# Output projection, second norm, queries and scores of a transformer-like block, cut into two halves of 256 tokens

## The chip, the cores and the metric

One core of one Trainium2 chip runs the whole block. The metric is the device time of one execution in microseconds (us). Its engines are TensorE (PE; PEld is its loading of weights), VectorE (DVE), ScalarE (ACT), GpSimd (POOL) and SyncE (SP), which issues most DMA transfers. Each works through its own list of instructions in order and waits for the others by semaphores.

## The reference

One layer on 512 tokens of width 1024, in float32. Cut to what this change touches:

```
y = concat([head_rmsnorm(y_a), head_rmsnorm(y_b)]) @ w_out     # output projection
x = x + g1 * y
h = modulate(rmsnorm(x, norm2_g), sh2, sc2)                    # second norm
q = (h @ w_q).reshape(p, 8, 2, 64)                             # queries: 8 heads, 2 halves of 64
sc = einsum('phcd,hcnd->phcn', q, sub_keys)                    # scores against 128 keys per half
top_s, top_i = top_k(sc, 16)                                   # stage 1 of the search
best_s, best_pos = top_k(all sums of a pair of them, 16)       # stage 2
idx = the 16 of 16384 experts per token and head;  g = softmax(best_s)
act = gelu(einsum('phkd,pd->phk', expert_u[idx], h))
x = x + g2 * einsum('phk,phkd->pd', g * act, expert_v[idx])
out = rmsnorm(x, final_g)
```

## The kernel before

Tokens stand in four tiles of 128. Activations are transposed: a tensor is [128 features, 8 blocks k, 512 tokens]. Each float32 product is made of three fast ones: `split_w` turns a 512 KB weight block (`wraw`) into a rounded part (`whi`, ACT, L76) and its remainder (`wlo`, DVE, L81), and `mm3` (L90 to L92) issues for each k whi times the rounded activation, whi times its remainder, and wlo times the rounded activation: 24 matmuls for a block. `wraw`, `whi` and `wlo` have four buffers each.

The program has these stages.

1. The mixer (to about 188 us), which this change leaves alone. It ends in `ybuf_h` and `ybuf_l`, the input of the output projection.
2. Output projection: a loop over 8 blocks m of features, 24 matmuls of 512 tokens each; DVE adds to the residual `xs` (L388); ACT squares it (L162) and DVE sums the squares (L164).
3. Second norm: PE sums the squares over the features (L154), `rsqrt_small` (L111 to L117, DVE and ACT) makes 1/rms, PE spreads it over the partitions (`ps_rs`, L172), and for each k DVE multiplies (L434), `modulate` scales and shifts (DVE L213, ACT L214, DVE L215), and PE transposes the result of tile 0 and of the first 64 tokens of tile 1 (L423, L425) to `h2n` and `h2b`, which the gathered tokens need. Meanwhile `xs` is transposed (L399) and stored for the end.
4. Queries and scores: a loop over 8 heads h, 24 matmuls of 512 tokens, an eviction of the query (`qT`, ACT L484), 8 score matmuls (L488) and two evictions of the scores (`sc`, ACT L494). DVE starts the searches of stage 1 there (`top16`, L451 to L460; one tile of one head is one item): heads 0 to 3, all four tiles, 16 items.
5. The u phase: 124 of 128 chunks of `expert_u`, 24 matmuls of 320 tokens each (`ps_act`, L90 to L92), ACT evicting with Gelu (L817). These are the dense tokens, 64 to 128 of tile 1 and tiles 2 and 3. Tile 0 and the first 64 tokens of tile 1 are instead gathered: POOL fetches the 128 rows of one chosen expert per token (L729, 512 KB), and DVE makes one "dot" of it (L750); 64 dots for tile 1 (index `idx_b`), then 128 for tile 0 (index `idx_s`). The other 16 items of stage 1, stage 2 (`topk_tile`) and the "gates" (which put the weights of the chosen experts in the dense layout: DVE L605 and L615, ACT L613, PE L621, 96 steps) run beside the chunks.
6. The v phase: the last four u chunks among 128 chunks of `expert_v`, 18 matmuls of 512 columns each (L996); beside them the dots that are left and 128 sums of gathered `expert_v` rows (DVE L766).
7. The end: the gated residual and the final norm.

Up to the end of stage 4 the order on each engine is made by a scheduler from the program's text. From stage 5 on it is a list made in Python (`manual_schedule`): a planner keeps estimated times of PE, DVE and ACT (`pe[0]`, `dve[0]`, `ac[0]`), and in each chunk lets `turn` choose pieces of searches ("s", "r"), gates ("g") and dots ("d") until DVE's estimate reaches PE's. Dots of tile 0 wait until `topk_tile(0)` has been placed (`sready`, L746), which comes after `topk_tile(1)`, the rest of stage 1, and `topk_tile(2)`. In the v phase, `share` spreads the steps that are left evenly over the chunks, whatever their number.

## Time and profile before

| | us |
|---|---|
| median of 3 runs | 1409.85 (1409.26 to 1412.09) |
| the profiled execution | 1409.24 |
| its span, from first to last instruction | 1407.5 |
| around the span | 1.74 |

| engine | busy us | share of the span |
|---|---|---|
| PE | 1357.2 | 96% |
| PEld | 1176.0 | 84% |
| DVE | 1231.5 | 87% |
| ACT | 735.2 | 52% |
| POOL | 540.1 | 38% |

The DMA queues moved 440.10 MB. Busy shares are means over stages with different limits, and a busy PE is not a PE at its peak, since a matmul's recorded length (390 ns at 512 columns) is longer than the distance between two of them (227 ns). So the prediction goes by starts, and by stage.

### The profile page before, as it was taken

The numbers are of one execution on the slowest core, as the hardware profiler recorded it, in microseconds if no ns is written. First come the engines' busy times: TensorE is split into PE (matmuls) and PEld (weight loads), VectorE is DVE, ScalarE is ACT, GpSimd is POOL, SyncE is SP. The second block draws the span as 40 slices with busy tenths as digits, with TensorE's granted clock in tenths as the row PEclk, the third lists the DMA queues.
The fourth block names the chain that finished last, engine by engine and source line by source line (L and its number), as shares of the span: only waits on it lengthen the run. The fifth ranks groups of instructions, "written<-read, shape, count | busy, mean of one in ns | idle before, by whom it ended". The sixth has DMA issues, their size and how long they took to land.

```text
span 1407.5 us, 22023 instructions
## 1 busy us (share of the span) xinstructions
PE 1357.2 (96%) x7739; PEld 1176.0 (84%) x7739; DVE 1231.5 (87%) x2470; ACT 735.2 (52%) x1212; POOL 540.1 (38%) x334
## 2 busy tenths in 40 slices
PE   5999998999999999999999989999999999999996
PEld 2566777779999999999999988877778888878884
DVE  6676565799999999989999967989989898999998
ACT  3554433536489699956996533333333333343342
POOL 0000000000135434514333335666757676766770
PEclk9999999999999999999999999999999999999998
DMA  9575323124689899978999899999999999999994
GB/s 378 213 256 197 132 85 103 53 91 138 206 273 406 320 346 367 391 251 309 353 369 373 301 402 383 368 359 413 410 413 414 415 412 415 414 407 413 414 369 177
DMA packets 146931, 440.10 MB, mean 313 GB/s; under 512 B 14722, under 2 KB 42370, under 8 KB 144772
## 3 DMA queue, kind: packets, MB, share of 16 engines
q1 hardware_dynamic: 99812, 267.75, 51.4%
q0 software_dynamic: 46720, 169.89, 31.5%
q8 instruction: 61, 1.00, 0.3%
q10 hardware_dynamic: 288, 1.05, 0.2%
q14 instruction: 50, 0.41, 0.1%
HBM read 393.54 MB, written 45.09 MB: 312 GB/s over the span
## 4 chain that ended last, share of the span: by engine, by line
PE 32%; issue 24%; DMA 20%; DVE 16%; POOL 6%; ACT 1%; DVEq 0%; POOLq 0%; SPq 0%; ACTq 0%
DMA wraw<-in_v_dram 13%; PE acc L996 7%; POOL rows L729 6%; PE ps_z L90 5%; PE ps_z L92 5%; PE ps_z L91 5%; DMA rows<-in_u_dram,idx_s 3%; DVE wlo L81 3%; DVE scr L750 3%; DVE ys L766 3%; DMA rows<-in_u_dram,idx_b 2%; PE ps_act L90 2%; DVE cf L882 2%; PE ps_act L91 2%; PE ps_act L92 2%
## 5 line engine op out<-in xcount | busy, mean ns | idle before, releaser
L76 ACT ACTIVATE whi<-wraw 128x1024 fp32r<-128x1024 f32 x292 | 308.4, 1057 | 392.9 <-DMA wraw<-in_v_dram 170.0
L81 DVE TENSOR_TENSOR wlo<-wraw,whi 128x1024 fp32r<-128x1024 f32 x292 | 356.1, 1221 | 82.5 <-ACT whi L76 81.3
L90 PE MATMUL ps_act<-h,whi 128*128 128x320 f32 x1024 | 322.4, 315 | 1.5 <-ACT sc L494 1.2
L91 PE MATMUL ps_act<-h,whi 128*128 128x320 f32 x1024 | 317.0, 310 | 0.0
L92 PE MATMUL ps_act<-h,wlo 128*128 128x320 f32 x1024 | 316.8, 309 | 0.0
L729 POOL DMA_INDIRECT rows<-in_u_dram,idx_s x128 | 201.1, 1571 | 226.5 <-DVE scr L750 187.3
L729 POOL DMA_INDIRECT rows<-in_v_dram,idx_s x128 | 234.7, 1833 | 108.9 <-DVE ys L766 82.1
L996 PE MATMUL acc<-whi,cl 128*128 128x512 f32 x750 | 232.7, 392 | 6.1 <-DVE cl L893 6.1
L996 PE MATMUL acc<-whi,ch 128*128 128x512 f32 x750 | 232.8, 391 | 5.2 <-ACT act L817 3.9
L996 PE MATMUL acc<-wlo,ch 128*128 128x512 f32 x750 | 232.0, 390 | 0.0
L90 PEld LDWEIGHTS ps_act<-h,whi 128*128 128x128 f32 x1024 | 193.0, 189 | 2.1 <-ACT sc L494 1.4
L91 PEld LDWEIGHTS ps_act<-h,whi 128*128 128x128 f32 x1024 | 193.0, 189 | 0.2
L92 PEld LDWEIGHTS ps_act<-h,wlo 128*128 128x128 f32 x1024 | 192.7, 188 | 0.0
L729 POOL DMA_INDIRECT rows<-in_u_dram,idx_b x64 | 99.2, 1550 | 211.7 <-DVE scr L750 105.6
L996 PEld LDWEIGHTS acc<-whi,cl 128*128 128x128 f32 x750 | 140.5, 189 | 38.8 <-DVE cl L893 10.2
L996 PEld LDWEIGHTS acc<-whi,ch 128*128 128x128 f32 x750 | 141.0, 188 | 35.7 <-ACT act L817 4.7
L996 PEld LDWEIGHTS acc<-wlo,ch 128*128 128x128 f32 x750 | 141.4, 189 | 29.7
L766 DVE SCALAR_TENSOR_TENSOR ys<-rows,acts,ys 128x1024 f32<-128x1024 f32 x127 | 162.8, 1282 | 1.6
L750 DVE SCALAR_TENSOR_TENSOR scr<-rows,h2n 128x1024 f16<-128x1024 f32 x128 | 156.4, 1222 | 8.2 <-DMA rows<-in_u_dram,idx_s 6.7
L406 POOL DMA_DIRECT2D x1d<-xn x8 | 4.6, 569 | 282.5 <-DVE wlo L81 234.9
L817 ACT ACTIVATE act<-ps_act 128x320 f32<-128x320 f32 x128 | 55.4, 433 | 102.3 <-PE ps_act L92 100.4
L621 PE MATMUL ps_gt<-igh,jh 128*128 128x128 f32 x768 | 97.4, 275 | 2.6 <-DVE igh L615 0.9
(258 smaller groups left out, 1888.4 us busy)
## 6 DMA issues: line engine op xcount, KB each, us to landing
wraw<-in_uT_dram SPq DMA_DIRECT2D x128, 512.0 KB, 6.8
wraw<-in_v_dram SPq DMA_DIRECT2D x128, 512.0 KB, 10.1
Gd<-stg SPq DMA_DIRECT2D x46, 512.0 KB, 7.0
wada<-in_w_ada_dram SPq DMA_DIRECT2D x16, 1024.0 KB, 5.3
Ad<-act SPq DMA_DIRECT2D x48, 320.0 KB, 7.7
act<-Ad SPq DMA_DIRECT2D x48, 320.0 KB, 11.4
h<-Gd SPq DMA_DIRECT2D x12, 1024.0 KB, 17.7
wraw<-in_w_in_dram SPq DMA_DIRECT2D x20, 512.0 KB, 6.0
```

Of the source, the lines that this page charges most:

```text
L76: nc.scalar.activation(hi, raw, AF.Copy)
L81: nc.vector.tensor_sub(lo, raw, hi.bitcast(F32))
L90: nc.tensor.matmul(ps, hi[:, k, :], xh(k), start=first and k == ks[0], stop=False)
L91: nc.tensor.matmul(ps, hi[:, k, :], xl(k), start=False, stop=False)
L92: nc.tensor.matmul(ps, lo[:, k, :], xh(k), start=False, stop=last and k == ks[-1])
L621: nc.tensor.matmul(pg[:, :, k], jh[:, k, :], ig[:, k, :], start=True, stop=True)
L729: nc.gpsimd.indirect_dma_start(out=r[:, :], out_offset=None, in_=table, in_offset=bass.IndirectOffsetOnAxis(ap=idxs[:, k:k + 1], axis=0))
L750: nc.vector.scalar_tensor_tensor(scr, rows.pop(n), 1.0, hn, op0=OP.mult, op1=OP.mult, accum_out=dst[:, k:k + 1])
L766: nc.vector.scalar_tensor_tensor(ys, rows.pop(k), acts[:, k:k + 1], ys, op0=OP.mult, op1=OP.add)
L817: nc.scalar.activation(act[c // 2][:, c % 2], ps, AF.Gelu)
L882: nc.vector.tensor_mul(cf[:, :, XB:].rearrange("p c (g t) -> p c g t", t=16), act.pop(vorder[2 * q] // 2).rearrange("p c (g t) -> p c g t" ...
L996: nc.tensor.matmul(accs[b][e], st[:, bs], mv[:, e * 512:(e + 1) * 512], start=first, stop=last)
```

## The change

- The tokens are cut into two halves of 256 (tiles 0 and 1, tiles 2 and 3). The output projection runs over all 8 blocks for half 0, then over all 8 for half 1. `w_out` is loaded and split twice.
- Statistic, 1/rms and modulation are made for each half. Those of half 0 are written in the text before the projection of half 1, those of half 1 before the queries.
- Queries and scores go in 16 steps of one head and 256 tokens: heads 0 to 3 of half 0, heads 0 to 3 of half 1, then the same for heads 4 to 7. `w_q` is split once: four heads' weights are kept for both halves.
- The 16 items searched during the queries are now tiles 1 and 0 of all eight heads, one item after each step from the second on. In the u phase `topk_tile(1)` comes first, and the rest of stage 1 is tiles 2 and 3 of all heads.
- The scores have a pool for each half, and no buffer of theirs is used twice. The pool `ring` moves to the other side of SBUF.

In the diff's core, lines of "..." mark what is left out:

```diff
-    def modulate(t1, k, A, B, hh, hl, full=None):
-        f = sq_pool.tile([128, T], F32, name="mfull")
+    def modulate(t1, k, A, B, hh, hl, full=None, cols=slice(0, T)):
+        f = sq_pool.tile([128, T], F32, name="mfull")[:, 0:cols.stop - cols.start]
         nc.vector.tensor_scalar(f, t1, A[:, k:k + 1], B[:, k:k + 1], op0=OP.mult, op1=OP.add)
-        nc.scalar.activation(hh[:, k, :], t1, AF.Identity, scale=A[:, k:k + 1], bias=B[:, k:k + 1])
-        nc.vector.tensor_sub(hl[:, k, :], f, hh[:, k, :].bitcast(F32))
+        nc.scalar.activation(hh[:, k, cols], t1, AF.Identity, scale=A[:, k:k + 1], bias=B[:, k:k + 1])
+        nc.vector.tensor_sub(hl[:, k, cols], f, hh[:, k, cols].bitcast(F32))
...
-    oraw = {0: load_w(w_out[0]), 1: load_w(w_out[1])}
-    for m in range(KB):
-        if m + 2 < KB:
-            oraw[m + 2] = load_w(w_out[m + 2])
-        hi, lo = split_w(oraw[m])
-        ps = psZ.tile([128, T], F32, name="ps_z", bufs=3)
-        mm3(ps, hi, lo, lambda k: ybuf_h[:, k, :], lambda k: ybuf_l[:, k, :], kord, True, True)
-        nc.vector.scalar_tensor_tensor(xs[:, m, :], ps, adac[:, 16 + m:17 + m], xs[:, m, :], op0=OP.mult, op1=OP.add)
-        sq_sum(m, True)
-    mx.close()
-    adx.close()
-    qp = pro.enter_context(tc.tile_pool(name="qp", bufs=2))
+    HT = T // 2
+    half_cols = [slice(HT * e, HT * (e + 1)) for e in range(2)]
+    oraw = {i: load_w(w_out[i]) for i in range(2)}
     x1d = dram.tile([T, D], F32, name="x1d")
+    rstd2 = const.tile([128, NT], F32, name="rstd2")
+    A2 = const.tile([128, KB], F32, name="A2")
+    h2n = persist.tile([128, D], F32, name="h2n")
+
+    def half_stat(pst, src, o, first, last):
+        for t in range(2):
+            nc.tensor.matmul(pst[:, t:t + 1], src[:, o + t * 128:o + (t + 1) * 128], ones,
+                             start=first and t == 0, stop=last and t == 1, skip_group_check=True)
+
+    def out_half(e):
+        cs_ = half_cols[e]
+        for m in range(KB):
+            i = KB * e + m
+            if i + 2 < 2 * KB:
+                oraw[i + 2] = load_w(w_out[(i + 2) % KB])
+            hi, lo = split_w(oraw.pop(i))
+            ps = psZ.tile([128, T], F32, name="ps_z", bufs=3)[:, 0:HT]
+            mm3(ps, hi, lo, lambda k: ybuf_h[:, k, cs_], lambda k: ybuf_l[:, k, cs_], kord, True, True)
+            xm = xs[:, m, cs_]
+            nc.vector.scalar_tensor_tensor(xm, ps, adac[:, 16 + m:17 + m], xm, op0=OP.mult, op1=OP.add)
+            if m == 0:
+                nc.scalar.activation(sqa[:, cs_], xm, AF.Square)
+                continue
+            sq = sq_pool.tile([128, T], F32, name="sq")
+            nc.scalar.activation(sq[:, 0:HT], xm, AF.Square)
+            if m < KB - 1:
+                nc.vector.tensor_add(sqa[:, cs_], sqa[:, cs_], sq[:, 0:HT])
+        pst = psA.tile([128, NT], F32, name="ps_col")[:, 0:2]
+        half_stat(pst, sqa, HT * e, True, False)
+        half_stat(pst, sq, 0, False, True)
+        rs = rstd2[:, 2 * e:2 * e + 2]
+        rsqrt_small(rs, pst, 1.0 / D, 2)
+        psr = psA.tile([128, T], F32, name="ps_rs")[:, 0:HT]
+        rows_of(psr, rs, 2)
+        return psr
...
-    rstd2 = const.tile([128, NT], F32, name="rstd2")
-    rsqrt_small(rstd2, pst, 1.0 / D, NT)
-    x1p = [x1_mm(0)]
-    psr2 = psA.tile([128, T], F32, name="ps_rs")
-    rows_of(psr2, rstd2)
-    x1p += [x1_mm(1), x1_mm(2)]
-    A2 = const.tile([128, KB], F32, name="A2")
-    nc.vector.scalar_tensor_tensor(A2, adac[:, 32:40], 1.0, sm("n2g"), op0=OP.add, op1=OP.mult)
-    h2n = persist.tile([128, D], F32, name="h2n")
-    sel = ctx.enter_context(tc.tile_pool(name="sel", bufs=1, side="right"))
-    h2b = sel.tile([128, D], F32, name="h2b")
+    def norm_half(e, psr, full):
+        for k in range(KB):
+            t1 = sq_pool.tile([128, T], F32, name="mt1")[:, 0:HT]
+            nc.vector.tensor_mul(t1, xs[:, k, half_cols[e]], psr)
+            modulate(t1, k, A2, adac[:, 24:32], h2h, h2l, full, half_cols[e])
...
     tp_cur = []
+    psr = out_half(0)
+    nc.vector.scalar_tensor_tensor(A2, adac[:, 32:40], 1.0, sm("n2g"), op0=OP.add, op1=OP.mult)
+    h2b = sel.tile([128, D], F32, name="h2b")
+    norm_half(0, psr, full2)
+    psr = out_half(1)
+    mx.close()
+    qp = pro.enter_context(tc.tile_pool(name="qp", bufs=2))
     qraw = {0: load_w(w_q[0]), 1: load_w(w_q[1])}
-    for k in range(KB):
-        t1 = sq_pool.tile([128, T], F32, name="mt1")
-        nc.vector.tensor_mul(t1, xs[:, k, :], psr2)
-        modulate(t1, k, A2, adac[:, 24:32], h2h, h2l, full2)
-        if k < 3:
-            x1_out(*x1p[k])
+    norm_half(1, psr, None)
     ep = ExitStack()
-    ring = ctx.enter_context(tc.tile_pool(name="ring", bufs=1, side="right"))
     scp = ep.enter_context(tc.tile_pool(name="scp", bufs=1, side="right"))
     top = scp.tile([128, NT, 8, 2, 16], F32, name="top")
     ti = scp.tile([128, NT, 8, 2, 16], U32, name="ti")
     scx = ExitStack()
-    scs = scx.enter_context(tc.tile_pool(name="scs", bufs=1, side="right"))
+    scs = [pro.enter_context(tc.tile_pool(name="sca", bufs=1)),
+           scx.enter_context(tc.tile_pool(name="scb", bufs=1, side="right"))]
...
-    def stage1(heads, tiles):
-        for t in tiles:
-            for h in heads:
-                yield from top16([(top[:, t, h, c], ti[:, t, h, c], sc[h, c][:, t, :]) for c in range(2)], 128, 1150)
+    def stage1(items):
+        for t, h in items:
+            yield from top16([(top[:, t, h, c], ti[:, t, h, c], sc[h, t // 2][:, c, t % 2, :]) for c in range(2)], 128, 1150)
     qsp = {}
-    early = chain(*(stage1([h], range(NT)) for h in range(HQ)))
-
-    for h in range(8):
-        if h + 2 < 8:
-            qraw[h + 2] = load_w(w_q[h + 2])
-        if h == 0:
-            qsp[0] = split_w(qraw[0])
-        if h + 1 < 8:
-            qsp[h + 1] = split_w(qraw[h + 1])
+
+    def q_split(h):
+        if h < 8 and h not in qsp:
+            for i in range(h, min(h + 3, 8)):
+                if i not in qraw:
+                    qraw[i] = load_w(w_q[i])
+            qsp[h] = split_w(qraw[h])
+
+    def q_step(e, h):
         hi, lo = qsp[h]
-        ps = psZ.tile([128, T], F32, name="ps_z", bufs=3)
-        mm3(ps, hi, lo, lambda k: h2h[:, k, :], lambda k: h2l[:, k, :], range(KB), True, True)
-        qT = qp.tile([128, T], F32, name="qT")
+        cs_ = half_cols[e]
+        ps = psZ.tile([128, T], F32, name="ps_z", bufs=3)[:, 0:HT]
+        mm3(ps, hi, lo, lambda k: h2h[:, k, cs_], lambda k: h2l[:, k, cs_], range(KB), True, True)
+        qT = qp.tile([128, HT], F32, name="qT")
         nc.scalar.activation(qT, ps, AF.Copy)
-        pss = [psZ.tile([128, NT, 128], F32, name="ps_g", bufs=2) for c in range(2)]
-        for t in range(NT):
+        pss = [psZ.tile([128, NT, 128], F32, name="ps_g", bufs=2)[:, 0:2] for c in range(2)]
+        for t in range(2):
             for c in range(2):
                 nc.tensor.matmul(pss[c][:, t, :], qT[64 * c:64 * c + 64, t * 128:(t + 1) * 128],
                                  keys_sb[64 * c:64 * c + 64, h, :], start=True, stop=True)
-        for _ in range(6 if h >= 2 else 0):
-            next(early, None)
+        sc[h, e] = scs[e].tile([128, 2, 2, 128], F32, name="sc", bufs=SCB)
         for c in range(2):
-            sc[h, c] = scs.tile([128, NT, 128], F32, name="sc", bufs=SCB)
-            nc.scalar.activation(sc[h, c], pss[c], AF.Copy)
-        if h + 3 < 8:
-            x1_out(*x1_mm(h + 3))
-    assert next(early, None) is None
+            nc.scalar.activation(sc[h, e][:, c], pss[c], AF.Copy)
+
+    early = stage1([(t, h) for h in range(8) for t in (1, 0)])
+    x1n = 0
+    for g in (0, 4):
+        for e in range(2):
+            for h in range(g, g + 4):
+                if e == 0:
+                    q_split(h)
+                if e or h % 4 < 3:
+                    q_split(h + (4 if e else 1))
+                q_step(e, h)
+                if (g, e, h) > (0, 0, 0):
+                    for _ in range(2):
+                        next(early)
+                if e and x1n < 8:
+                    x1_out(*x1_mm(x1n))
+                    x1n += 1
+    for _ in early:
+        pass
...
+    ring = ctx.enter_context(tc.tile_pool(name="ring", bufs=1))
...
     def searches_E():
-        heads = range(HQ, 8)
-        yield from stage1(heads, [1])
         yield from topk_tile(1)
         sready.append(1)
         while not gopen:
...
     def rest_E():
-        yield from stage1(range(HQ, 8), [2, 0, 3])
+        yield from stage1([(t, h) for t in (2, 3) for h in range(8)])
         scx.close()
```

Three places in the instruction lists show what moved. The first is PE at the change from the output projection (`ybuf`) to the queries (h_82 is the normalised input). Before:

```order
L92 MATMUL ps_z<-ybuf_h,wlo 128x512
L154 MATMUL ps_col<-ones,sqa 128x1 x4
L399 MATMUL ps_z<-ident,xs 128x128 x12
L154 MATMUL ps_col<-ones,sq 128x1 x4
L172 MATMUL ps_rs<-ident,rstd_1842 128x128 x4
L90 MATMUL ps_z<-h_82,whi 128x512
```

And now, in half 1:

```order
L92 MATMUL ps_z<-ybuf_h,wlo 128x256
L389 MATMUL ps_col<-ones,sqa 128x1 x2
L90 MATMUL ps_z<-h_82,whi 128x256
L91 MATMUL ps_z<-h_82,whi 128x256
L92 MATMUL ps_z<-h_82,wlo 128x256
L90 MATMUL ps_z<-h_82,whi 128x256
```

The statistic, which stood alone between projection and queries, now stands among the query matmuls of half 0; that of half 0 stands in the same way among the projection of half 1.

The second is DVE at the end of the queries: the remainders `wlo` of the first u chunks, and the searches of stage 1 (`top`, `ti`). Before:

```order
L460 MAX_INDEX ti<-top,rep 128x8 x2
L81 TENSOR_TENSOR wlo<-wraw,whi 128x1024 x3
L451 MAX top<-sc 128x8 x2
L453 MAX_INDEX ti<-top,sc 128x8 x2
L455 MATCH_REPLACE rep<-top,sc 128x128 x2
```

Now:

```order
L477 MAX top<-rep 128x8 x2
L479 MAX_INDEX ti<-top,rep 128x8 x2
L81 TENSOR_TENSOR wlo<-wraw,whi 128x1024 x3
L566 TENSOR_TENSOR cand<-top 128x8x16
L566 TENSOR_TENSOR cand<-top 128x8x24
```

The three remainders have moved behind the last of the 16 early items, and stage 2 of tile 1 (`cand`) follows them at once.

The third is DVE in the u phase, just before the index of tile 0 is made (`oh` belongs to `topk_tile(0)`). Before:

```order
L750 SCALAR_TENSOR_TENSOR scr,act_b<-rows,h2b 128x1024 x2
L81 TENSOR_TENSOR wlo<-wraw,whi 128x1024
L750 SCALAR_TENSOR_TENSOR scr,act_b<-rows,h2b 128x1024
L81 TENSOR_TENSOR wlo<-wraw,whi 128x1024
L750 SCALAR_TENSOR_TENSOR scr,act_b<-rows,h2b 128x1024
L81 TENSOR_TENSOR wlo<-wraw,whi 128x1024
L569 TENSOR_TENSOR oh<-oh,st_2604 128x2048
```

Now:

```order
L782 SCALAR_TENSOR_TENSOR scr,act_b<-rows,h2b 128x1024
L81 TENSOR_TENSOR wlo<-wraw,whi 128x1024 x3
L603 TENSOR_TENSOR oh<-oh,st_3192 128x2048
L604 TENSOR_TENSOR oh<-oh,dif 128x2048
L607 TENSOR_TENSOR oh<-oh 128x128x8
```

The dots of tile 1 now run out earlier, so that two chunks' remainders follow each other with no dot between. Counted in chunks (one `wlo` each, from the first u chunk), the first dot stands behind the 22nd remainder before and behind the 18th now, the index of tile 0 behind the 77th before and the 79th now, and behind the 124th stand 114 dots before and 110 now. Behind the 111th stand 98 and 97.

More of the change, by code (lines that the diff above doesn't have):

```diff
@@ L155, in stat, with sq_sum @@
                              start=first and t == 0, stop=last and t == NT - 1, skip_group_check=True)
-    def sq_sum(k, split):
+    def sq_sum(k):
         if k == 0:
@@ L162, in sq_sum, with rows_of @@
         nc.scalar.activation(sq, xs[:, k, :], AF.Square)
-        if k < KB - 1 or not split:
-            nc.vector.tensor_add(sqa, sqa, sq)
+        nc.vector.tensor_add(sqa, sqa, sq)
         if k == KB - 1:
-            stat(sqa, True, not split)
-            if split:
-                stat(sq, False, True)
-    def rows_of(ps, rstd):
-        for t in range(NT):
+            stat(sqa, True, True)
+    def rows_of(ps, rstd, n=NT):
+        for t in range(n):
             nc.tensor.matmul(ps[:, t * 128:(t + 1) * 128], rstd[:, t:t + 1].to_broadcast([128, 128]), ident,
@@ L175, in block_kernel @@
     for k in range(KB):
-        sq_sum(k, False)
+        sq_sum(k)
     rstd1 = const.tile([128, NT], F32, name="rstd1")
@@ L376, in block_kernel @@
     head_norm(*pend.pop())
-    pst = psA.tile([128, NT], F32, name="ps_col")
+    adx.close()
+    sel = ctx.enter_context(tc.tile_pool(name="sel", bufs=1, side="right"))
     kord = [4, 0, 5, 1, 6, 2, 7, 3]
-    oraw = {0: load_w(w_out[0]), 1: load_w(w_out[1])}
-    for m in range(KB):
-        if m + 2 < KB:
-            oraw[m + 2] = load_w(w_out[m + 2])
-        hi, lo = split_w(oraw[m])
-        ps = psZ.tile([128, T], F32, name="ps_z", bufs=3)
-        mm3(ps, hi, lo, lambda k: ybuf_h[:, k, :], lambda k: ybuf_l[:, k, :], kord, True, True)
-        nc.vector.scalar_tensor_tensor(xs[:, m, :], ps, adac[:, 16 + m:17 + m], xs[:, m, :], op0=OP.mult, op1=OP.add)
-        sq_sum(m, True)
@@ L463, in block_kernel @@
     sc = {}
-    def stage1(heads, tiles):
-        for t in tiles:
-            for h in heads:
-                yield from top16([(top[:, t, h, c], ti[:, t, h, c], sc[h, c][:, t, :]) for c in range(2)], 128, 1150)
+    def stage1(items):
+        for t, h in items:
+            yield from top16([(top[:, t, h, c], ti[:, t, h, c], sc[h, t // 2][:, c, t % 2, :]) for c in range(2)], 128, 1150)
     qsp = {}
-    early = chain(*(stage1([h], range(NT)) for h in range(HQ)))
-    for h in range(8):
-        if h + 2 < 8:
-            qraw[h + 2] = load_w(w_q[h + 2])
-        if h == 0:
-            qsp[0] = split_w(qraw[0])
-        if h + 1 < 8:
-            qsp[h + 1] = split_w(qraw[h + 1])
+    def q_split(h):
[5 more added lines that the diff above has]
+    def q_step(e, h):
         hi, lo = qsp[h]
-        ps = psZ.tile([128, T], F32, name="ps_z", bufs=3)
-        mm3(ps, hi, lo, lambda k: h2h[:, k, :], lambda k: h2l[:, k, :], range(KB), True, True)
-        qT = qp.tile([128, T], F32, name="qT")
+        cs_ = half_cols[e]
+        ps = psZ.tile([128, T], F32, name="ps_z", bufs=3)[:, 0:HT]
+        mm3(ps, hi, lo, lambda k: h2h[:, k, cs_], lambda k: h2l[:, k, cs_], range(KB), True, True)
+        qT = qp.tile([128, HT], F32, name="qT")
         nc.scalar.activation(qT, ps, AF.Copy)
-        pss = [psZ.tile([128, NT, 128], F32, name="ps_g", bufs=2) for c in range(2)]
-        for t in range(NT):
+        pss = [psZ.tile([128, NT, 128], F32, name="ps_g", bufs=2)[:, 0:2] for c in range(2)]
+        for t in range(2):
             for c in range(2):
@@ L1100 @@
 SCB = 8
-HQ = 4
 VT = 3
```

## The prediction

> **What bounds the kernel now.** I read the page's engine line first, then a table of windows cut where stages begin, then the timeline of PE at the seams, then waits and DMA of the v phase. The windows show, for each stretch, its length and then the busy time of PE, PEld, DVE, ACT and POOL, the granted clock, the DMA share and GB/s:
>
> ```profile
> span 1407.5 us, 22023 instructions
> 187.84:233.80 45.96, 45.96 (x218) 37.50 (x217) 22.65 (x32) 14.74 (x20) 0.00 (x0) 1.00 0.30 93
> 233.80:262.03 28.23, 24.12 (x130) 17.29 (x128) 17.64 (x33) 13.52 (x22) 2.39 (x4) 0.88 0.17 57
> 262.03:310.10 48.07, 45.46 (x289) 36.27 (x288) 47.87 (x283) 21.17 (x34) 2.16 (x4) 1.00 0.28 90
> 310.10:844.00 533.90, 527.51 (x3756) 525.25 (x3756) 501.21 (x1283) 386.31 (x731) 183.73 (x119) 1.00 0.88 317
> 844.00:1381.00 537.00, 529.12 (x2345) 436.64 (x2345) 495.20 (x539) 204.32 (x263) 351.22 (x201) 1.00 1.02 401
> 1381.00:1407.50 26.50, 12.81 (x57) 10.29 (x55) 22.59 (x56) 7.33 (x21) 0.00 (x0) 0.83 0.29 106
> ```
>
> The rows are the output projection, the norm with the first two heads' queries, the other queries, the u phase, the v phase, the end. PE is busy almost everywhere, so what the change touches is worth what it takes from or adds to PE's line between 187.84 and 310.10, and after that only what reaches PE through a wait. PE's starts at the seam after the projection:
>
> ```profile
> 233.79 0.95 PE L154 MATMUL ps_col<-ones,sqa 128*128 128x1 f32 x8
> 236.44 1.05 PE L154 MATMUL ps_col<-ones,sq 128*128 128x1 f32 x8 [0.33 <-ACT sq L162]
> 238.99 1.16 PE L172 MATMUL ps_rs<-ident,rstd 128*128 128x128 f32 x8 [1.50 <-DVE rstd L117]
> 242.43 0.79 PE L90 MATMUL ps_z<-h,whi 128*128 128x512 f32 x1 [2.28 <-ACT h L214]
> 246.79 0.63 PE L90 MATMUL ps_z<-h,whi 128*128 128x512 f32 x1
> 247.22 0.63 PE L91 MATMUL ps_z<-h,whi 128*128 128x512 f32 x1
> 249.33 0.39 PE L91 MATMUL ps_z<-h,whi 128*128 128x512 f32 x1
> 250.76 0.50 PE L92 MATMUL ps_z<-h,wlo 128*128 128x512 f32 x1
> ```
>
> PE waits 0.33 + 1.50 + 2.28 = 4.1 us for the norm, and then runs slowly for some microseconds: 0.43 us between matmuls at 246.79, where it is 0.227 at full clock (below).
>
> **The change part by part.** *Matmuls of half the width.* Two rows of the projection that are 24 matmuls apart, and the evictions of two u chunks of 24 matmuls:
>
> ```profile
> 228.13 0.39 PE L92 MATMUL ps_z<-ybuf_h,wlo 128*128 128x512 f32 x1
> 233.57 0.39 PE L92 MATMUL ps_z<-ybuf_h,wlo 128*128 128x512 f32 x1
> 322.31 0.44 ACT L817 ACTIVATE act<-ps_act 128x320 f32<-128x320 f32 x1 [2.14 <-PE ps_act L92]
> 325.83 0.44 ACT L817 ACTIVATE act<-ps_act 128x320 f32<-128x320 f32 x1 [2.13 <-PE ps_act L92]
> ```
>
> That is 5.44/24 = 0.2267 us at 512 columns and 3.52/24 = 0.1467 at 320. The straight line through both gives 0.120 at 256. Projection and queries go from 2 x 192 matmuls (87.1 us) to 2 x 384 (92.2): **+5.1 us**. The ends are 0 (half of 0.2267 each) and +25.6 (0.1467 each, a floor that the 320 row would then be). I take the line, because its fixed part, 0.0134 us, is small at both widths.
>
> The Trainium skill (TensorE: Matmul & The Clock Gate, section Back-to-back issue gap) gives N/2.4 + 2.5 ns for a single matmul's gap, 109 ns at 256 columns; by it the halving would cost 1.0 us, and the sum would end 4.1 us lower. Its 215.8 ns at 512 and 135.8 at 320 both lie 11 ns under the rows here, so I keep the rows.
>
> *Score blocks.* Sixteen blocks of 4 score matmuls replace eight of 8:
>
> ```profile
> 294.36 1.16 PE L488 MATMUL ps_g<-keys_sb,qT 64*128 64x128 f32 x16
> 301.12 1.16 PE L488 MATMUL ps_g<-keys_sb,qT 64*128 64x128 f32 x16
> 307.77 1.16 PE L488 MATMUL ps_g<-keys_sb,qT 64*128 64x128 f32 x16 [1.41 <-ACT qT L484]
> 310.10 0.63 PE L90 MATMUL ps_act<-h,whi 128*128 128x320 f32 x1 [1.17 <-ACT sc L494]
> ```
>
> A head takes 6.76 us, of which 5.44 are its 24 matmuls, so a block costs 1.32. If all of it scales, nothing is added; if only the 0.95 of its 16 passes does (0.059 each), 8 x 0.37 = 3.0 are. I take **+2.5**. The second statistic and spread of 1/rms add two switches: **+0.5**, ends 0 and 1.
>
> *The seam.* From 233.80 to 262.03 stand 48 query matmuls (10.9 us), eight transposes for the gathered tokens (1.43 - 0.23 = 1.2 for two, so 4.8), 13 transposes of xs (1.2) and the statistics (2.3): 19.2 us of work in 28.23. The 9.0 lost are the 4.1 of waits and 4.9 of slow clock (0.88 over the window). After the change PE has the projection of half 1 to do while half 0 is normalised, and four heads of half 0 while half 1 is: **-9.0**. The cover: half 1's norm must be ready four steps after the projection, 4 x (24 x 0.120 + 0.82) = 14.8 us. DVE's part is about 5.5 us to its first product (6.4 in the rows from 233.79, with slow clock) and eight blocks of about 1 us, 13.5 in all. Were it late, each microsecond would return as a wait. DVE's unit costs:
>
> ```profile
> L434 DVE TENSOR_TENSOR mt<-xs,ps_rs 128x512 f32<-128x512 f32 x8 | 5.1, 682 | 1.2 <-PE ps_rs L172 1.2
> L215 DVE TENSOR_TENSOR h<-mfull,h 128x512 fp32r<-128x512 f32 x16 | 10.7, 689 | 2.4 <-ACT h L214 2.3
> L81 DVE TENSOR_TENSOR wlo<-wraw,whi 128x1024 fp32r<-128x1024 f32 x292 | 356.1, 1221 | 82.5 <-ACT whi L76 81.3
> 268.79 0.47 DVE L451 MAX8 top<-sc 128x8 f32<-128x128 f32 x2
> 271.13 0.47 DVE L451 MAX8 top<-sc 128x8 f32<-128x128 f32 x2
> ```
>
> The eight added loads and splits of w_out cost nothing on PE: a block lasts 2.88 us, and DVE needs 1.22 for the remainder and about 0.7 for the halved sums, ACT 1.06 and 0.3, DMA 512 KB (180 GB/s, where the window moved 93). In half 1 DVE's blocks and the norm come to 16 + 10 us in 30.
>
> *The end of the queries.* PE waited 1.41 + 1.17 us there, and the first u chunk began at half clock. With evictions half as long I take **-1.5**, ends 0 and -2.6. The three first u remainders now stand behind all searches, so the u phase waits if DVE is late: 16 items of 2.34 us (271.13 - 268.79), seven remainders, the norm, together 13.5 + 37.4 + 8.5 = 59 us after the projection, against PE's 16 x 3.70 + 8 transposes of 0.45 + 1.6 = 64. Covered by 5 us; without cover the difference would be paid.
>
> *New waits* (the first blocks of half 0 reach the last head norm's result sooner, evictions queue behind ACT's modulation): **+0.7**, ends 0 and 3. Up to the u phase the sum is 5.1 + 2.5 + 0.5 - 9.0 - 1.5 + 0.7 = **-1.7 us**.
>
> *The u phase.* Work per chunk is the same. Dots begin four chunks sooner, but the 64 of tile 1 are done before the index of tile 0 exists, and that index comes two chunks later than before; so DVE has nothing to fill two chunks with, and 110 dots instead of 114 are done when 124 chunks' weights are. I take **0** for PE (ends -1 and +1), which waits little for gates there.
>
> *The v phase* inherits those 4 dots, each a fetch of 512 KB and about 1.2 us of DVE. What bounds it:
>
> ```profile
> DMA packets 30760, 82.52 MB, mean 413 GB/s; under 512 B 2526, under 2 KB 11770, under 8 KB 30748
> 970.00:980.00 10.00, 8.78 (x39) 6.77 (x37) 7.98 (x12) 2.14 (x3) 7.45 (x5) 1.00 1.04 412
> 1100.00:1200.00 100.00, 100.00 (x442) 82.68 (x442) 94.10 (x88) 40.23 (x51) 68.15 (x37) 1.00 1.03 414
> ACT whi L76 <- DMA wraw<-in_v_dram: 169.4, 63, 8.0
> PE acc L996 <- DVE cl L893: 6.1, 8, 2.2
> ```
>
> The first line is the DMA of 1100 to 1300: 413 GB/s, with a share above 1. The window of 970, where PE has gaps, moves no more (412) than that of 1100, where it has none. So DMA is full in both. At 413 GB/s the phase's 537 us x 401 GB/s = 215 MB need 521 us; PE's 2345 matmuls (96 of them at 0.1467) need 524; together they took 537. Four fetches more are 2.1 MB, 5.1 us if DMA alone sets the pace, 0 if PE does. I take **+3**, nearer to the upper end because DMA never rests.
>
> The Trainium skill (DMA: Bandwidth & Descriptors, section Measured) lists 425 GB/s for one core's large loads; by it DMA would have 3% in hand, and the sum would lack these 3 us. No window of this trace longer than 5 us shows more than 418, so I keep the row.
>
> **The sum.** -1.7 + 0 + 3 = +1.3 on the profiled execution's 1409.24: 1410.5. The median before lies 0.6 above that execution, so I predict **1411 us**: no change that can be told, since a measurement of this kernel tells about 0.2%, 2.8 us.
>
> **The rivals.** *Slower by the v phase (chance 0.25).* DMA is the bound through the whole phase: +5.1, and with half of what the new waits may cost (+1.5 for 0.7) the sum is +4.2, 1413.4 or 1414 as a median. It decides where four fetches no longer fit, at more than 413 GB/s of demand, which is what 1100 to 1300 already shows. Against it: PE had no wait in 1100 to 1200. *Slower by the remainders (0.08).* DVE comes to the first u remainder after PE; if the norm's half-width operations cost as much as the full ones (8 x 1.9 instead of 8 x 1), DVE needs 66 us against 64, with waits for scores 70: the u phase begins 6 us later than in my sum, 1417. For it: DVE was busy 47.87 of 48.07 us in the queries before. Against it: it started its items later then. *Faster (0.22).* Halving costs PE nothing (0 for the +5.1 and for the +2.5), the seam goes in full: -9.3 before the u phase, and with +3 behind it 1403.5 as a median; with half of these savings 1407. For it: the lower ends are not excluded by any row at 256 columns. *It does not do what it says:* the searches of the gathered tokens do all run early, yet the fetches gain nothing because tile 0 waits; that is in my forecast.
>
> **Chances and range.** No change 0.45, the two slower cases 0.33, faster 0.22. The likeliest case's own range is 1407 to 1412.7. To hold 8 in 10 it must reach to the middle of both sides: **1405 to 1416.5**.
>
> **What would show it.** Right: matmuls at 256 columns 0.12 us apart; no PE wait above 0.5 us between projection and queries, clock 1.00 there; the first u matmul at 307 to 309.5; stage 2 of tile 1 on DVE before PE's first u chunk ends; a v phase of 538 to 542 us with the same 413 GB/s. Wrong: 256-column matmuls at 0.147 or at 0.113; PE waiting for `wlo` at the first u chunk; a v phase that is shorter, or longer by more than 5 us; a u phase that differs by more than 2 us.

## The result: slower by a third to a half of a per cent

The changed kernel took 1417.22 us as a median of four runs (1414.42 to 1419.36), beside 1409.55 for the kernel before on the same chip: a ratio of 1.0051, with an interval of 1.0028 to 1.0074. Run again with five rounds it came to 1415.49 (1413.47 to 1416.57) beside 1410.20, 1.0033 with an interval of 1.0021 to 1.0045. So it is slower, by 5 to 8 us; the forecast was 1411 and "no change".

The profiled executions lie 5.2 us apart (1414.42 and 1409.24). The windows of the changed kernel, cut at its own stages; the columns are those of the table before the change:

```profile
span 1412.7 us, 22901 instructions
187.73:310.78 123.05, 120.94 (x1018) 112.38 (x1016) 104.55 (x426) 63.41 (x123) 4.55 (x8) 1.00 0.36 119
310.78:844.63 533.85, 526.41 (x3755) 525.05 (x3755) 495.43 (x1257) 376.58 (x712) 170.98 (x115) 1.00 0.88 312
844.63:1381.00 536.37, 528.58 (x2325) 434.87 (x2326) 495.78 (x542) 202.93 (x260) 341.52 (x205) 0.99 1.02 403
1381.00:1412.70 31.70, 17.28 (x77) 13.90 (x75) 27.73 (x61) 9.44 (x24) 0.00 (x0) 0.85 0.37 143
```

Projection to queries last 123.05 us where the three rows of before give 122.26, with the granted clock at 1.00. In the u phase DMA moved 312 GB/s, where it was 317. The end, from 1381, is 5.2 us longer: what was lost was lost ahead of it. Five points of PE's and VectorE's timelines place it (us from the start of the span):

| point | before | changed | changed, again |
|---|---|---|---|
| first u matmul | 310.10 | 310.78 | 310.48 |
| last matmul of the u phase | 839.45 | 839.27 | 839.22 |
| first v matmul | 843.22 | 844.63 | 844.34 |
| last v matmul | 1393.42 | 1397.89 | 1398.06 |
| end of the last VectorE operation | 1404.17 | 1409.37 | 1409.57 |

From row to row the first profile of the change gains or loses: +0.7 up to the u phase, -0.9 in it, +1.6 at the seam to the v phase (5.36 us instead of 3.77), +3.1 in the v phase, +0.7 at the end. Together 5.2.

In the first half, the matmuls of 256 columns and the score blocks of the changed kernel, and the last PE waits before the u phase:

```profile
200.10 0.28 PE L90 MATMUL ps_z<-ybuf_h,whi 128*128 128x256 f32 x1
202.98 0.28 PE L90 MATMUL ps_z<-ybuf_h,whi 128*128 128x256 f32 x1
280.46 0.71 PE L507 MATMUL ps_g<-keys_sb,qT 64*128 64x128 f32 x8
284.30 0.71 PE L507 MATMUL ps_g<-keys_sb,qT 64*128 64x128 f32 x8
309.32 0.71 PE L507 MATMUL ps_g<-keys_sb,qT 64*128 64x128 f32 x8 [0.86 <-ACT qT L503]
310.78 0.58 PE L90 MATMUL ps_act<-h,whi 128*128 128x320 f32 x1 [0.74 <-ACT sc L511]
```

The first two rows are 24 matmuls apart: 2.88/24 = 0.120 us each. A head without transposes of xs takes 3.84 us, so a score block of 8 passes costs 3.84 - 2.88 = 0.96, where one of 16 had cost 1.32. The two waits at the end, 1.6 us, are all that is left of PE's waits between the projection and the u phase.

At the seam between the phases, first the kernel before, then the changed one (ScalarE's copy of a later u chunk's weights, which stands in its list ahead of the eviction `act`, and PE's first v matmuls):

```profile
840.71 1.06 ACT L76 ACTIVATE whi<-wraw 128x1024 fp32r<-128x1024 f32 x1 [7.52 <-DMA wraw<-in_uT_dram]
843.22 0.80 PE L996 MATMUL acc<-whi,ch 128*128 128x512 f32 x1 [3.46 <-ACT act L817]
844.49 0.80 PE L996 MATMUL acc<-whi,ch 128*128 128x512 f32 x1 [0.48 <-ACT act L817]
```

```profile
842.13 1.06 ACT L76 ACTIVATE whi<-wraw 128x1024 fp32r<-128x1024 f32 x1 [7.84 <-DMA wraw<-in_uT_dram]
844.63 0.80 PE L1028 MATMUL acc<-whi,ch 128*128 128x512 f32 x1 [5.05 <-ACT act L849]
846.87 0.80 PE L1028 MATMUL acc<-whi,ch 128*128 128x512 f32 x1 [1.45 <-ACT act L849]
```

ScalarE waits for a weight load in both, and PE behind it; in the changed kernel the load lands 1.4 us later. That points at DMA. Its line for the stretch from 310 to 840 us, before and changed:

```profile
DMA packets 51173, 167.91 MB, mean 317 GB/s; under 512 B 5371, under 2 KB 8443, under 8 KB 51119
```

```profile
DMA packets 50337, 164.94 MB, mean 311 GB/s; under 512 B 5290, under 2 KB 8343, under 8 KB 50284
```

By 840 us the changed kernel has moved 3.0 MB less. A whole run of it moves 4.2 MB more (444.3 for 440.1), `w_out` a second time, but that comes before 310 us: from there to the end the two move the same, 387.3 and 387.5 MB. So the 3.0 MB are still to come, in a phase that moves 413 GB/s where DMA is full: 7.2 us of DMA time. Four dots' fetches are 2.1 MB of it.

### The profile page after: what moved, and what is told of

It is laid out like the page before. It is cut to its first block, busy times and chain, and to the rows that moved or that the text cites. A ratio compares the mean times of both kernels' runs of the same rounds, so it can differ in the third digit from the quotient of the medians.

```text
span 1412.7 us, 22901 instructions
## 1 busy us (share of the span) xinstructions
PE 1364.5 (97%) x8123; PEld 1198.2 (85%) x8123; DVE 1247.8 (88%) x2531; ACT 740.1 (52%) x1243; POOL 517.7 (37%) x334
## 4 chain that ended last, share of the span: by engine, by line
PE 35%; issue 28%; DMA 14%; DVE 14%; POOL 7%; ACT 2%; DVEq 0%; SPq 0%; POOLq 0%; ACTq 0%
DMA wraw<-in_v_dram 11%; POOL rows L761 7%; PE acc L1028 6%; PE ps_z L91 5%; PE ps_z L92 5%; PE ps_z L90 5%; DVE ys L798 3%; PE ps_act L90 3%; PE ps_act L91 3%; PE ps_act L92 3%; DVE scr L782 3%; DVE wlo L81 2%; DVE cf L914 2%; DVE cl L925 2%; DMA rows<-in_u_dram,idx_s 1%
## 5 line engine op out<-in xcount | busy, mean ns | idle before, releaser
L76 ACT ACTIVATE whi<-wraw 128x1024 fp32r<-128x1024 f32 x300 | 316.7, 1056 | 375.7 <-DMA wraw<-in_v_dram 183.9
L81 DVE TENSOR_TENSOR wlo<-wraw,whi 128x1024 fp32r<-128x1024 f32 x300 | 365.4, 1220 | 84.3 <-ACT whi L76 83.1
L761 POOL DMA_INDIRECT rows<-in_v_dram,idx_s x128 | 217.3, 1698 | 121.2 <-DVE ys L798 94.1
L761 POOL DMA_INDIRECT rows<-in_u_dram,idx_b x64 | 93.3, 1458 | 195.0 <-DVE scr L782 125.3
L90 PE MATMUL ps_z<-h,whi 128*128 128x512 f32 (+1 forms) x288 | 102.1, 356 | 2.4 <-ACT h L211 1.9
```

Source lines behind the costliest of these rows:

```text
L76: nc.scalar.activation(hi, raw, AF.Copy)
L81: nc.vector.tensor_sub(lo, raw, hi.bitcast(F32))
L90: nc.tensor.matmul(ps, hi[:, k, :], xh(k), start=first and k == ks[0], stop=False)
L761: nc.gpsimd.indirect_dma_start(out=r[:, :], out_offset=None, in_=table, in_offset=bass.IndirectOffsetOnAxis(ap=idxs[:, k:k + 1], axis=0))
```

## The experiments

Five theories stood against each other. **A**: the change loses because fetches move into the v phase, where DMA is the bound. **B**: the halves themselves lose, whatever the search items. **C**, **F**: PE or VectorE, not DMA, sets the pace there. **D**: the new order stalls the u phase. **E**, **G**: the loss is at the seam. The counts of dots in the expectations (113 and 109) count those that stand ahead of the 124th remainder; the text on the change counts one more. Each ratio is against the kernel before, on the same chip.

### The changed kernel once more

> The changed kernel once more, beside the other kernels of this group. Both theories expect what it showed: 1414 to 1419 us, median near 1417, where before is near 1409.5. Its first profile was of its fastest execution (1414.42). If that profile tells all there is, this one shows the first u chunk at 310.8 us, the first v matmul at 844.6, the last v matmul at 1397.9; if the other executions lose 3 us more in one place, a profile of about 1417 shows where.

1415.49 us, 1.0033 (1.0021 to 1.0045). Its profile, of an execution of 1414.63 us, is the last column of the table above and has the same steps: +0.4, -0.6, +1.4, +3.5, +0.8. The 1417 us of the first group did not come back, and no profile was taken of an execution that long; what the further 2 to 3 us of those runs were stays open.

### One half of the change at a time

The change does two things: it halves the width of projection, norm, queries and scores, and it chooses other items for the early searches. Each was run alone. Only the halves, on the changed kernel ("..." marks what is left out):

```diff
-        sc[h, e] = scs[e].tile([128, 2, 2, 128], F32, name="sc", bufs=SCB)
+        sc[h, e] = scs[h // 4].tile([128, 2, 2, 128], F32, name="sc", bufs=SCB)
...
-    early = stage1([(t, h) for h in range(8) for t in (1, 0)])
+    early = stage1([(t, h) for h in range(4) for t in (0, 1)] + [(t, h) for h in range(4) for t in (2, 3)])
...
     def searches_E():
+        yield from stage1([(1, h) for h in range(4, 8)])
...
     def rest_E():
-        yield from stage1([(t, h) for t in (2, 3) for h in range(8)])
+        yield from stage1([(t, h) for t in (2, 0, 3) for h in range(4, 8)])
```

> Only the halves: projection, norm, queries and scores in two halves of 256 tokens as in the changed kernel, but the sixteen early search items are those of before (all four tiles of heads 0 to 3), so that the searches, gates and dots of the u phase stand in the order of before, with 113 dots behind the 124th remainder where the changed kernel has 109. Theory A (the loss comes from the four dots that move into a v phase bound by DMA): the u phase begins 0.7 us later than before, the v phase is that of before, 1409.5 to 1411.5 us. Rival B (the loss comes from the halves, whatever the items): 1415 to 1418 us.

1410.30 us, 1.0005 (0.9995 to 1.0014): no difference that can be told. In its profile the u phase begins at 310.65 us, 0.55 later than before. B falls: what the halves cost PE in matmuls and score blocks they get back at the norm, to within a microsecond. One thing in this profile (of an execution of 1411.51 us) matters below: the seam to the v phase lasts 5.58 us, as long as in the changed kernel (5.36 and 5.12), although no dot has moved. Behind the seam it takes 551.0 us from the first to the last v matmul, where the changed kernel takes 553.3 and 553.7.

Only the items, on the kernel before (queries at full width; the scores are kept in half tiles so that they fit, which is two copies more on ScalarE for each head; "..." marks what is left out):

```diff
-    scs = scx.enter_context(tc.tile_pool(name="scs", bufs=1, side="right"))
+    scs = [pro.enter_context(tc.tile_pool(name="sca", bufs=1)),
+           scx.enter_context(tc.tile_pool(name="scb", bufs=1, side="right"))]
...
-    early = chain(*(stage1([h], range(NT)) for h in range(HQ)))
+    early = stage1([(t, h) for h in range(8) for t in (1, 0)])
...
-        for _ in range(6 if h >= 2 else 0):
+        for _ in range(4 if h >= 1 else 0):
             next(early, None)
...
-        yield from stage1(range(HQ, 8), [2, 0, 3])
+        yield from stage1([(t, h) for t in (2, 3) for h in range(8)])
```

> Only the choice of early items: projection, norm and queries at full width as before, but the sixteen early items are tiles 1 and 0 of all eight heads, and the u phase stands in the order of the changed kernel (109 dots behind the 124th remainder). The scores are copied out by half tiles, two copies more for each head. Theory A: four fetches of 512 KB and 1.3 us of DVE each move to the v phase, 1413 to 1417 us. Rival B: 1409 to 1411 us.

1420.83 us, 1.0077 (1.0064 to 1.0091): above A's range, and twice the loss of the changed kernel on the same chip (5.3). The surplus is at the start of the u phase, where this kernel's PE waits; the last row is ScalarE's:

```profile
306.35 1.16 PE L487 MATMUL ps_g<-keys_sb,qT 64*128 64x128 f32 x16 [1.41 <-ACT qT L483]
308.81 0.41 PE L90 MATMUL ps_act<-h,whi 128*128 128x320 f32 x1 [1.29 <-ACT sc L494]
322.03 0.41 PE L92 MATMUL ps_act<-h,wlo 128*128 128x320 f32 x1 [2.10 <-DVE wlo L81]
329.99 0.64 PE L90 MATMUL ps_act<-h,whi 128*128 128x320 f32 x1 [4.48 <-ACT act L817]
323.72 1.91 ACT L566 ACTIVATE oh<-pf 128x2048 f16<-128x2048 f16 x1 [7.13 <-DVE pf L556]
```

At full width the last head's score matmuls begin 2.5 us before the first u chunk, VectorE still has that head's tiles 1 and 0 to search, and a remainder of the first chunks is late (2.10 us). The longer wait, 4.48 us, is for an eviction: ScalarE stands for 7.13 us at a step of tile 1's stage 2, which VectorE feeds, and the eviction stands behind that. From its first to its last matmul the u phase takes 535.6 us, 7.1 more than the changed kernel's 528.5; it begins 2.0 sooner, so 5.1 us are lost there. That is the prediction's rival of the late remainders, with the eviction as the larger part. The changed kernel is spared it: there the last block that the early items need is that of head 7's first half, at 291.98 us, 18.8 us ahead of the first u chunk:

```profile
291.98 0.71 PE L507 MATMUL ps_g<-keys_sb,qT 64*128 64x128 f32 x8
```

So the halves make the new items bearable, and the new items are what costs: the halves alone can't be told from no change, and the items on top of them cost about 5 us (1415.49 against 1410.30, on one chip).

### What a dot costs in the v phase

Two kernels hold dots of the kernel before back, eleven and four of them, and change nothing else:

```diff
         for n, (_, hn, dst, k) in enumerate(usteps):
+            while n >= 102 and cur[0] < CE - 1:
+                yield None
```

(109 for 102 in the second.)

> The kernel before, but the dots stop at 102 until the last u chunk of the u phase, so that 11 dots more are done in the v phase; nothing else is changed. This measures the price of a dot that moves from the u to the v phase. Theory A (DMA at 413 GB/s sets the pace there): 11 x 1.27 us = 14 us, so 1421 to 1425 us, the u phase as before. Rival C (PE sets the pace, and DMA and DVE have room): 0 to 4 us, 1409 to 1414 us.

> The kernel before, but the dots stop at 109 until the last u chunk, so that four of them, which stood at the last chunks of the u phase, are done in the v phase. The same count as in the changed kernel, with nothing else of it. Eleven dots held back had cost 8.5 us, 0.77 each. Theory A: 3 to 5 us, 1413 to 1415.5 us. Rival E (the stall at the seam between the phases comes from the fetches of those last dots, and goes with them, as it went with eleven held back: first v matmul at 839 us where it was 843): the gain of the seam pays for the four, 1408 to 1411 us.

Eleven cost 8.5 us (1418.75; 1.0060, 1.0046 to 1.0073), four 2.4 (1412.07; 1.0017, 1.0005 to 1.0030): less than A alone expected, more than C or E. Both profiles show why. First the PE rows of the one with 109 around the seam and its window of 840 to 870 us, then that window of the kernel before:

```profile
839.23 0.40 PE L998 MATMUL acc<-whi,ch 128*128 128x512 f32 x1
839.92 0.50 PE L998 MATMUL acc<-whi,ch 128*128 128x512 f32 x1 [0.29 <-ACT act L819]
840.00:870.00 30.00, 30.00 (x166) 27.13 (x167) 22.10 (x29) 11.55 (x15) 13.35 (x10) 1.00 0.90 336
```

```profile
840.00:870.00 30.00, 26.30 (x129) 23.03 (x130) 22.67 (x28) 13.39 (x19) 13.65 (x10) 0.89 1.01 375
```

With the last four fetches put off, the stall at the seam is gone: the first v matmul comes 4.0 us sooner and the clock stays at 1.00. But first to last v matmul then takes 556.6 us, 6.4 more than 550.2. What was saved at the seam was DMA work put off. With eleven held back it is -4.1 and +13.95, 1.27 us a dot, which is 512 KB at 413 GB/s. Over the whole run a dot cost less, 0.77 us of eleven and 0.6 of four, since the seam gave a part back. In the kernel before DMA's share is 1.03, 1.06 and 1.01 from 800 to 820, to 840 and to 870 us, so the seam is a part of the stretch in which DMA is full. With the dots held back it is not full there (0.90 from 840 to 870 us): what was left undone then is what the v phase pays.

### Which engine is behind: a fetch left out, a sum left out

Both kernels are the changed one. The first leaves out 4 of the 128 fetches of value rows but sums a tile in their place; the second fetches them and leaves out the sums:

```diff
             for kk in range(k, min(k + ahead() - 1, 128)):
+                if kk in (32, 56, 80, 104):
+                    rows[kk] = h2n
                 gath(v, idx_s, kk, kk)
```

```diff
+            if k in (32, 56, 80, 104):
+                rows.pop(k)
-            if k == 0:
+            elif k == 0:
```

> The changed kernel, with 4 of the 128 fetches of value rows in the v phase left out; their sums are done on a tile that is already there, so that VectorE has the same work and the sums of the gathered tokens are not the reference's. Theory A with DMA as the bound: 4 x 512 KB at 413 GB/s are 5.1 us, 1410 to 1412.5 us. Rival F (VectorE's chain of remainders and sums is the bound): within 1.5 us of the changed kernel, 1414 to 1417 us.

> The changed kernel, with the same 4 of the 128 value rows fetched as ever, but not summed: VectorE has 4 operations of 1.28 us less, DMA the same bytes; the sums of the gathered tokens are not the reference's. Theory A with DMA as the bound: within 1.5 us of the changed kernel, 1414 to 1417 us. Rival F (VectorE is the bound): 4 x 1.28 = 5.1 us less, 1410 to 1412.5 us.

Without four fetches 1411.17 us, 1.0007 (0.9994 to 1.0020): the loss is gone but for 1 us. Without four sums 1415.85 us, 1.0040 (1.0027 to 1.0054): nothing gained. The two ran on one chip and lie 4.7 us apart, where A had 5.1. In the profile without four sums VectorE's last sum ends 2.1 us sooner than in the repeated profile of the changed kernel (1387.41 for 1389.53), but that execution was itself 2.1 us shorter (1412.51 for 1414.63), so the row doesn't tell. In the profile without four fetches 2.9 us of the gain on the first profile of the change lie between the first and the last v matmul; 1.8 lie in the u phase, which the edit leaves alone, and show how far two executions differ. The chain that ended last agrees with the medians: from 1200 us to the end PE's v matmuls are 36% of it in the kernel before and 39% without four fetches, but 2% or nothing in the changed kernel, in its repeat and without four sums, where loads of weights (13 to 34%) and VectorE's operations stand on it.

F falls, and A holds where it matters: the fetches in the v phase set the time of this kernel. Two things stay open. A fetch left out takes its instruction on GpSimd with it, so the bytes are not tested apart from that engine; for the bytes speak DMA's share of 1.03 and GpSimd's 64 busy us of 100 (from 1100 us). And in the changed kernel's first profile that chain is VectorE's from 1305 us on, while three of the four sums stand ahead of it; of that last stretch their run says little.

### Giving the dots back

If fetches ahead of the v phase are what lacks, an order that does more of them should mend it. First, tile 0's last search stage ahead of tile 2's, so that the dots don't wait for its index:

```diff
+        yield from topk_tile(0)
+        sready.append(0)
         yield from topk_tile(2)
-        yield from topk_tile(0)
-        sready.append(0)
```

> The changed kernel, but the gathered tokens' last search stage (tile 0) stands ahead of tile 2's, so that their index is ready 28 chunks sooner (behind the 51st remainder, not the 79th) and 113 dots stand behind the 124th remainder as before, not 109. Theory A (the change loses by four dots that move into the v phase): 1409 to 1411.5 us, the v phase as before. Rival D (the order of the u phase costs something else, and the gates of tile 2, which now come later, stall it): the u phase is over 2 us longer, 1413 to 1417 us.

1413.08 us, 1.0016 (1.0002 to 1.0030): about half the loss is back, not all. Its v phase is that of before (550.8 us from the first to the last matmul), so the dots did what A says; but the seam is worse:

```profile
847.05 0.80 PE L1028 MATMUL acc<-whi,ch 128*128 128x512 f32 x1 [6.67 <-ACT act L849]
848.32 0.80 PE L1028 MATMUL acc<-whi,ch 128*128 128x512 f32 x1 [0.48 <-ACT act L849]
```

Its DMA line for 310 to 840 us says how far it was:

```profile
DMA packets 50559, 166.43 MB, mean 314 GB/s; under 512 B 5331, under 2 KB 8195, under 8 KB 50506
```

1.5 MB less than before, though the count of dots is the same. The gathers' queue is 0.15 MB of that (62.12 for 62.27 MB), the queue of the weights' loads and the gates' stores 1.3 (102.59 for 103.91): counting dots was too narrow.

Then the planner's budget. RHO = 1.02 lets VectorE be given 2% more work than PE's time; with it the changed kernel, the one with tile 0 first, and the halves alone were run. A3 = 1000 instead has ScalarE take over gate operands.

```diff
-RHO = 1.0
+RHO = 1.02
```

> The changed kernel, with the planner of the u phase told that VectorE may do 2% more than PE's time (RHO 1.02 for 1.0): 118 dots behind the 124th remainder where the changed kernel has 109 and the kernel before 113; the gates' first operands are shared out nearly as in the kernel before (209 on VectorE for 215). Theory A (DMA bounds the v phase; a dot done before it saves 1.2 us, until PE is the bound): 9 x 1.2 = 11 us less at most, about 7 if PE's own work caps it, so 1405 to 1410 us. Rival D (VectorE has no room in the u phase, and PE waits there for remainders or gates): the u phase is longer by more than 3 us, 1414 to 1420 us.

> The changed kernel with both: tile 0's last search stage ahead of tile 2's, and RHO 1.02; 120 dots behind the 124th remainder. With tile 0 first alone the time was 3.3 us above the kernel before, although the count of dots was that of before, and the first v matmul came at 847 us, not 843. Theory A: seven dots more than that, 1404 to 1409 us. Rival G (what is lost with tile 0 first is the seam, where the later gates' stores and loads meet the last dots' fetches, and more dots there make it worse): the first v matmul at 847 us or later, 1412 to 1417 us.

> Only the halves, with the early items of before, and RHO 1.02 (118 dots behind the 124th remainder, where the kernel before has 113). The halves alone came out at 1.0005 of the kernel before, and RHO 1.02 took 3 us from the changed kernel. Theory A (a dot that is done before the v phase saves up to 1.2 us, less what VectorE then lacks in the u phase, 2.6 us there): five dots, 0.997 to 0.999 of before, 1405.5 to 1408.5 us. Rival D (the longer u phase takes all of it): 1409 to 1412 us.

> The changed kernel, with the limit from which ScalarE takes three of four of a gate step's second operands moved from 2000 to 1000 ns (169 on VectorE for 215); VectorE then does 127 dots by the 124th remainder, 18 more than the changed kernel. Theory A: the gain ends where PE is the bound, near 8 to 10 us, 1404 to 1409 us. Rival D (ScalarE, which is 19.5 of 20 us busy where the gates are made, holds up PE's gate products): ps_gt waits of more than 10 us, 1415 to 1425 us.

RHO took the changed kernel to 1412.25 (1.0009, 0.9997 to 1.0020), tile 0 first with it to 1410.16 (1.0003, 0.9991 to 1.0015), and the halves alone to 1409.68 (1.0001, 0.9991 to 1.0010). None of them is faster than the kernel before. The first two gain, as A said, but less, and their times lie in neither theory's range; the halves alone can't be told from what they were, which is D's range (1409 to 1412) and not A's. What limits them is the u phase: with RHO 1.02 its last matmul comes at 844.27, 842.34 and 841.68 us, 5.0, 2.3 and 2.2 later than in the same kernel without it. In the first that is more than the 3 us of D, and yet the time is below D's, since the v phase is 5.8 us shorter (547.5 for 553.3). The first v matmul of the second of them, at 846.78, is about as late as G expected, and yet the time is not.

A3 lost 19 us (1428.70; 1.0121, 1.0097 to 1.0144), more than D's range. D's waits are there, but with VectorE rather than ScalarE at their head; PE's longest waits in this kernel up to 830 us and behind it, and two of its gate steps on the timeline:

```profile
PE ps_gt L655 <- DVE jh L639: 12.3, 5, 5.6
PE ps_gt L655 <- DVE igh L649: 6.9, 15, 0.5
...
836.09 1.17 PE L655 MATMUL ps_gt<-igh,jh 128*128 128x128 f32 x8 [0.46 <-DVE igh L649]
837.71 1.17 PE L655 MATMUL ps_gt<-igh,jh 128*128 128x128 f32 x8 [0.46 <-DVE igh L649]
```

The 6.9 us are fifteen waits of about 0.46 us between gate steps that follow each other every 1.63 us, from 829.6 to 854.9 us, with no matmul of the weights between them: the gates did not get done in time and stood alone at the end of the phase.

### The bytes of all runs

What each kernel had moved from 310 to 840 us, by the line quoted above, against its time. The third column is the deficit against the kernel before at 413 GB/s:

| kernel | MB by 840 us | deficit, us | measured less before, us |
|---|---|---|---|
| before | 167.91 | 0 | 0 |
| items only | 162.92 | 12.1 | 10.6 |
| changed | 164.94 | 7.2 | 7.7 |
| changed, again | 165.29 | 6.3 | 5.3 |
| changed, four sums left out | 165.48 | 5.9 | 6.1 |
| changed, four fetches left out | 165.82 | 5.1, less 5.1 left out | 1.4 |
| dots held at 102 | 165.29 | 6.3 | 8.5 |
| tile 0 first | 166.43 | 3.6 | 3.3 |
| halves only | 166.96 | 2.3 | 0.1 |
| dots held at 109 | 167.16 | 1.8 | 2.3 |
| changed, RHO 1.02 | 167.44 | 1.1 | 2.7 |
| changed, A3 = 1000 | 168.05 | -0.3 | 19.2 |
| halves only, RHO 1.02 | 168.67 | -1.8 | -0.5 |
| tile 0 first, RHO 1.02 | 169.96 | -5.0 | 0.6 |

A deficit is paid, to within 2.2 us either way. That is also the scatter of one profile: the changed kernel, its repeat and the two with something left out do the same up to 840 us, and span 0.9 MB, 2.1 us. A3's loss is not one of bytes but of the gates. A surplus earns less than its size, clearly so in the last row only (5.0 us, and 0.6 lost): PE's own matmuls, 524 us of 537 in the v phase before, and a u phase that ends some 2 us later stand against it. The table is a correlation; the four fetches left out are the test of it (2.1 MB, and 3.7 to 6.2 us by the two ratios of the changed kernel).

## Why the prediction was wrong, step by step

- **Matmuls of half the width, +5.1:** right. 0.120 us each, as the line through 512 and 320 columns gave.
- **Score blocks, +2.5:** mis-sized. A block of 8 passes costs 0.96 us, so sixteen cost 15.4 where eight of 16 passes cost 10.6: +4.8. The two sizes give 0.045 us a pass and 0.60 that is fixed. My upper end, +3.0, took 0.059 for a pass, from its own duration in the row, and so only 0.37 for what every block pays again.
- **The seam after the projection, -9.0, the end of the queries, -1.5, and new waits, +0.7:** right together. The stretch grew by 0.8 us; less 5.1, 4.8 and the 0.5 that I had put for the second statistic (no row here gives it) that leaves -9.6 for the three, where the sum had -9.8. No PE wait is left at the norm, and the clock is 1.00. The u phase began 0.7 us later instead of 1.7 sooner, nearly all of it the score blocks.
- **The u phase, 0:** right for PE's matmuls (-0.9), but this was the step that hid the loss. I followed what PE waits for, and the four dots; I did not ask what DMA had moved by the end of it. That was 2.6 to 3.0 MB less.
- **The v phase, +3:** this is the step that failed. I had DMA at its bound from the first to the last window, four fetches worth 5.1 us, and then took +3, between that and nothing, since PE's matmuls alone need 524 us there. Alone the v phase grew by 3.1 and 3.5, as said; but time was also lost at the seam before it (+1.6 and +1.4) and behind it (+0.7 and +0.8), which the sum had at nothing. Together these are 5.4 and 5.6 us from the u phase's last matmul to the end, about the full price of the four fetches (5.1), which I had worked out as the upper end and given to a rival. That it is this sum exactly is in part luck: the seam is as long with the halves alone, where no dot has moved (5.58 us), so its part is not shown to be the dots'. One reading was wrong: that no window longer than 5 us shows more than 418 GB/s. From 1060 to 1066 us it is 421; but no window of 100 us passes 414, so the sum does not hang on it.
- **The rivals.** The slower one by the v phase (1414, chance 0.25) is what happened, in mechanism, and in place but for the seam; its 4.2 us fall 1 us short of the 5.2 between the profiled executions. The remainders (0.08) were late only where the halves were taken away. Faster did not come: halving had its price.
- **The miss added up:** the profiled execution took 1414.42 us where the sum had 1410.5, 3.9 more. Of these 2.4 lie ahead of the u phase, nearly all in the score blocks, -0.9 in the u phase, 0.1 in the v phase, and 2.3 at the seam and the end. So the score blocks cost the forecast as much as the seam and the end did. The 2.8 us from there to the first median, 1417.22, show in no profile.
- **The range:** it ended at 1416.5; the first median, 1417.22, lay above it, and the repeated one, 1415.49, in it.

## What to carry to other kernels

Where a later phase is bound by DMA from end to end, the unit to plan in is bytes moved before it begins: an order that leaves DMA idler earlier is paid back there, here at between half of the full rate (0.6 us for each of four dots held back) and all of it, whatever it saves on the engine that looks busiest. Work that a change starts sooner helps only if the work that depends on it can start sooner too: here the gathered tokens' first searches came early while the index they lead to came two chunks later. And splitting a tile in two pays every fixed part twice: here 5.1 us over 768 matmuls of 256 columns, and nearly as much, 4.8, over only sixteen small blocks between them.

## What the runs showed of the hardware that was not expected

Two short waits close together slowed PE's clock where a longer single one did not. The changed kernel, and the kernel before, at the same place in the v phase:

```profile
928.71 0.73 PE L1028 MATMUL acc<-whi,ch 128*128 128x512 f32 x2 [0.77 <-ACT ch L918]
931.58 0.80 PE L1028 MATMUL acc<-whi,cl 128*128 128x512 f32 x2 [1.67 <-DVE cl L925]
932.18 1.06 PE L1028 MATMUL acc<-whi,ch 128*128 128x512 f32 x2
933.03 1.06 PE L1028 MATMUL acc<-wlo,ch 128*128 128x512 f32 x2
935.56 0.62 PE L1028 MATMUL acc<-wlo,ch 128*128 128x512 f32 x2
```

```profile
929.19 0.74 PE L996 MATMUL acc<-whi,cl 128*128 128x512 f32 x2 [2.17 <-DVE cl L893]
929.77 0.63 PE L996 MATMUL acc<-whi,ch 128*128 128x512 f32 x2
930.24 0.62 PE L996 MATMUL acc<-wlo,ch 128*128 128x512 f32 x2
```

After 0.77 and 1.67 us, 2.9 us apart, two matmuls take 0.85 us instead of 0.46 for about 3.4 us: 1.6 us lost beside the 2.4 of waiting. After a single wait of 2.17 us nothing slows. Two waits are not enough by themselves either: in the kernel before 0.35 and 1.01 us, 2.2 us apart (1040.12 and 1042.33), slow nothing, while in the changed kernel 0.26 and 1.33, 2.5 us apart (973.61 and 976.14), do. The Trainium skill (TensorE: Matmul & The Clock Gate, section Part 1: The HAM clock gate) has the clock fall after an idle window of about 3.4 us, and rise again after a busy one of that length. The trace agrees with the second, by the 3.4 us of the slow stretch. It does not agree with the first as it stands, since no wait here was that long; what exactly is counted can't be told from these rows.
